# Gradient along rows: DMA issues moved from SyncE to GpSimd, row ends from GpSimd to VectorE

## The chip, the core and the metric

The kernel runs on one core of a Trainium2 chip. The metric is the device time of one execution in microseconds (us), the median of several runs. In the profile, DVE is VectorE, POOL is GpSimd, SP is SyncE, and SPq is the sequencer of SyncE that issues DMAs. 16 DMA engines move data between HBM (the input and the output) and SBUF (the memory on the core).

## The reference

```python
def setup_inputs():
    return {"x": np.random.randn(8192, 8192).astype(np.float32)}

def reference(x):
    return np.gradient(x, axis=1)
```

Along each row of 8192 values, every inner output is half the difference of its two neighbours, (x[j+1] - x[j-1]) / 2. The first output of a row is x[1] - x[0] and the last is x[8191] - x[8190], both without the half. The input is 268.4 MB and the output as much, and there is one subtraction for each value: each byte is read once and written once.

## The kernel before

The 8192 rows are worked in 32 sets. A set is 128 partitions by R = 2 rows, so that each partition holds W = 2 x 8192 values, 64 KB that lie side by side in HBM; a set is 8.39 MB. The sets come in groups of NB = 3 (the last group has two), and there are three buffers, `slot0` to `slot2`, one for each set of a group. A set is loaded to an offset of SH = 64 values in its slot, and the result is written from offset 0 of the same slot, so that the output lies behind the input that is still to be read.

Each set goes through five steps:

1. `load(i)` (line 55) brings the set in. It waits for the store of set i - 3, which used the slot before.
2. The row ends (line 65): one subtraction over four values in each partition, two for each of the two rows, into `ends`, a small tile with room for all sets. It runs on GpSimd and waits for the load.
3. The long instruction (line 71), on VectorE: half the difference of two shifted views of the whole slot, 16382 values in each partition. It ignores the borders of rows, so that the values at row ends come out wrong, and it overwrites the input. It waits for step 2.
4. The placing (line 82): a copy of the four row ends over the wrong values. It runs on VectorE for 20 of the sets, and on GpSimd for the 12 in which `i % 5` is 1 or 3 (the last two sets aside).
5. The store (line 84) takes the slot to the output; it waits for step 4.

The order on each engine is the order in which the program names its instructions (it is scheduled by hand), and an engine's queue works in that order. The three loads of the first group are issued first. After that come the steps of the three sets of a group, and once the third store of a group has been issued, the three loads of the next group follow, each after the store that frees its slot. All loads and stores stand in SyncE's queue, in this order:

```
L0 L1 L2 | S0 S1 S2 | L3 L4 L5 | S3 S4 S5 | ... | L30 L31 | S30 S31
```

The helper `chain` names the steps that an instruction has to wait for, so that the overlapping views of a slot bring in no other waits.

Of the kernel before, what the change touches and what calls it, by code (L numbers as in the profile page):

```python
# [1 line left out]

# [4 lines left out]


@with_exitstack
def kernel(  # L10
    ctx: ExitStack,
    tc: tile.TileContext,
    x: bass.AP,
    out: bass.AP,
):
    nc = tc.nc
    P = nc.NUM_PARTITIONS
    n, m = x.shape
    R = 2
    NB = 3  # L20
    SH = 64
    W = R * m
    nsets = n // (P * R)
    f32 = x.dtype

    def sets(a):
        found = []
        for first in range(0, nsets, NB):
            q = min(NB, nsets - first)
            rows = a[first * P * R : (first + q) * P * R, :].rearrange("(p q) m -> p (q m)", p=P)  # L30
            found += [rows[:, k * W : (k + 1) * W] for k in range(q)]  # L31
        return found

    x_sets, out_sets = sets(x), sets(out)

    pool = ctx.enter_context(tc.tile_pool(name="pool", bufs=1))
    pad = pool.tile([P, 32], f32, name="pad", tag="pad")
    slots = [pool.tile([P, SH + W], f32, name=f"slot{k}", tag=f"slot{k}") for k in range(NB)]
    ends = pool.tile([P, nsets, R, 2], f32, name="ends", tag="ends")
    loads, stores = [], [None] * nsets  # L40
    in_front = {}

    def chain(i, ins, *needed):
        group, engine = f"slot{i % NB}", ins.ins.engine
        keep = [o.ins for o in needed]
        if in_front.get(engine, (None,))[0] == group:
            keep.append(in_front[engine][1])
        tc.declare_no_dep(ins.ins, group=group, keep=keep, reason="implied by the needed step")
        tc.add_to_no_dep_group(group, ins.ins)
        in_front[engine] = group, ins.ins  # L50
        return ins

    def load(i):
        b = slots[i % NB]
        ins = nc.sync.dma_start(out=b[:, SH : SH + W], in_=x_sets[i])  # L55
        loads.append(chain(i, ins, *([stores[i - NB]] if i >= NB else [])))

    with tc.manual_schedule():
        for i in range(NB):
            load(i)  # L60
        for i in range(nsets):
            b = slots[i % NB]
            xin = b[:, SH : SH + W].rearrange("p (t m) -> p t m", m=m)

            ins = nc.gpsimd.tensor_sub(  # L65
                out=ends[:, i, :, :],
                in0=xin[:, :, 1 : m : m - 2],
                in1=xin[:, :, 0 : m - 1 : m - 2],
            )
            at = [chain(i, ins, loads[i])]  # L70
            ins = nc.vector._custom_dve(  # L71
                dve_ops.TENSOR_TENSOR_REDUCE_SUB_MAX,
                out=b[:, 1 : W - 1],
                in0=b[:, SH + 2 : SH + W],
                in1=b[:, SH : SH + W - 2],
                s0=0.0,
                s1=0.5,
            )
            halved = chain(i, ins, *at)
            res = b[:, 0:W].rearrange("p (t m) -> p t m", m=m)  # L80
            placer = nc.gpsimd if i % 5 in (1, 3) and i < nsets - 2 else nc.vector
            ins = placer.tensor_copy(out=res[:, :, 0 : m : m - 1], in_=ends[:, i, :, :])  # L82
            placed = chain(i, ins, halved)
            ins = nc.sync.dma_start(out=out_sets[i], in_=b[:, 0:W])
            stores[i] = chain(i, ins, placed)
            if i % NB == NB - 1:
                for k in range(i + 1, min(i + 1 + NB, nsets)):
                    load(k)


# [1 line left out]
_INS = ['x']  # L92
_OUTS = [((8192, 8192), 'float32')]


# [23 lines left out]
```

## Time and profile before

| | |
|---|---|
| time, median of 3 runs | 1245.82 us (1245.47 to 1245.9) |
| the profiled execution | 1246.23 us, of which 1244.3 us are the profile's span |
| VectorE busy | 554.6 us, 52 instructions |
| GpSimd busy | 8.9 us, 48 instructions |
| bytes moved by DMA | 536.88 MB, 431 GB/s over the span |
| long instruction on VectorE (line 71) | 32 of 17.224 us each |
| row ends on GpSimd (line 65) | 32 of 0.200 us each |
| placing on VectorE and on GpSimd (line 82) | 20 of 0.172 us and 12 of 0.192 us |
| from issue to landing, median | loads 57.9 us, stores 40.4 us |

How to read it: the span runs from the first to the last recorded instruction of one execution, and times in the timeline count from its start. A group of instructions has its line in the kernel, its engine, its output and input with their shapes, its count, its busy time and the mean of one, and the idle time of the engine ahead of it with what ended that. The time from issue to landing of a transfer includes its wait behind other transfers. A DMA record is one contiguous piece on one of the 16 engines; "GB/s" of a stretch counts the pieces that start in it, so that over a stretch of a few microseconds it can exceed what the engines carry or be zero while they are busy.

### The profile page before, as it was taken

What the parts mean: (1) busy time and instruction counts of PE and PEld (TensorE: products, weight loads), DVE (VectorE), ACT (ScalarE), POOL (GpSimd) and SP (SyncE); (2) the same over time, 40 slices, a digit from 0 to 9 for tenths busy, and PEclk for the clock granted to TensorE, in tenths of its full rate; (3) what the DMA queues carried; (4) which work ended last, traced back from release to release, by engine and by line L of the source; (5) the groups of instructions that cost most, each with busy time, mean ns of one, the idle gap of its engine ahead of it and who ended that gap; (6) DMA issues with size and microseconds to landing.
All of it is one profiled execution on the core that took longest, in us unless ns stands there. A gap on an engine that the chain in (4) does not pass through costs nothing.

```text
span 1244.3 us, 237 instructions
## 1 busy us (share of the span) xinstructions
DVE 554.6 (45%) x52; POOL 8.9 (1%) x48
## 2 busy tenths in 40 slices
DVE  2850583069009603850582079009603840591082
POOL 0000000000000000000000000000000000000000
DMA  9999999999999999999999999999999999999999
GB/s 404 438 436 423 421 438 438 438 438 436 434 423 430 434 438 438 430 436 432 428 434 436 432 436 434 438 436 430 432 428 438 436 434 438 434 434 430 430 409 404
DMA packets 9217, 536.88 MB, mean 431 GB/s; under 512 B 1024, under 2 KB 1024, under 8 KB 1024
## 3 DMA queue, kind: packets, MB, share of 16 engines
q1 hardware_dynamic: 9216, 536.88, 99.8%
q14 instruction: 1, 0.01, 0.0%
HBM read 268.44 MB, written 268.44 MB: 431 GB/s over the span
## 4 chain that ended last, share of the span: by engine, by line
another core or an unknown queue 74%; DVE 18%; DMA 3%; issue 2%; POOL 1%; SPq 0%; POOLq 0%
DVE slot L71 18%; DMA slot<-in_x_dram 3%; POOL ends L65 0%; POOL slot L82 0%; SPq L55 0%; POOLq L114 0%; DVE slot L82 0%
## 5 line engine op out<-in xcount | busy, mean ns | idle before, releaser
L71 DVE CUSTOM_DVE_ANT_0 slot<-slot 128x16382 f32<-128x16382 f32 x32 | 551.2, 17224 | 667.2 <-POOL ends L65 667.2
L65 POOL TENSOR_TENSOR ends<-slot 128x4 f32<-128x4 f32 x32 | 6.4, 200 | 988.1 <-DMA slot<-in_x_dram 988.1
L82 POOL COPY slot<-ends 128x4 f32<-128x4 f32 x12 | 2.3, 192 | 207.9 <-DVE slot L71 207.9
L82 DVE COPY slot<-ends 128x4 f32<-128x4 f32 x20 | 3.4, 172 | 0.7
L103 POOL MEMSET const-bfloat16-1.0<- 128x1 bf16 x1 | 0.1, 102 | 0.0
L103 POOL MEMSET const-uint8-127<- 128x1 uint8 x1 | 0.1, 102 | 0.0
L103 POOL MEMSET const-float32-0.0<- 128x1 f32 x1 | 0.1, 99 | 0.2 <-issue 0.2
L103 POOL MEMSET const-float32-1.0<- 128x1 f32 x1 | 0.1, 99 | 0.0
## 6 DMA issues: line engine op xcount, KB each, us to landing
slot<-in_x_dram SPq DMA_DIRECT2D x32, 57.9
out_dram<-slot SPq DMA_DIRECT2D x32, 40.4
```

What stands on the lines that cost most here:

```text
L65: ins = nc.gpsimd.tensor_sub(out=ends[:, i, :, :], in0=xin[:, :, 1 : m : m - 2], in1=xin[:, :, 0 : m - 1 : m - 2],)
L71: ins = nc.vector._custom_dve(dve_ops.TENSOR_TENSOR_REDUCE_SUB_MAX, out=b[:, 1 : W - 1], in0=b[:, SH + 2 : SH + W], in1=b[:, SH : SH + W - 2],
L82: ins = placer.tensor_copy(out=res[:, :, 0 : m : m - 1], in_=ends[:, i, :, :])
L103: nc = _bacc.Bacc("TRN2", target_bir_lowering=False, num_devices=1)
```

## The change

[...] The subtraction for the row ends and all placings run on VectorE. The order of the loads and stores among themselves, the sizes of the transfers, the slots and the waits for data stay as they were. SyncE's queue holds no transfer any more, and GpSimd's holds nothing but the 64 transfers.

```diff
     def load(i):
         b = slots[i % NB]
-        ins = nc.sync.dma_start(out=b[:, SH : SH + W], in_=x_sets[i])
+        ins = nc.gpsimd.dma_start(out=b[:, SH : SH + W], in_=x_sets[i], single_packet=True)
         loads.append(chain(i, ins, *([stores[i - NB]] if i >= NB else [])))
...
-            ins = nc.gpsimd.tensor_sub(
+            ins = nc.vector.tensor_sub(
                 out=ends[:, i, :, :],
...
             res = b[:, 0:W].rearrange("p (t m) -> p t m", m=m)
-            placer = nc.gpsimd if i % 5 in (1, 3) and i < nsets - 2 else nc.vector
-            ins = placer.tensor_copy(out=res[:, :, 0 : m : m - 1], in_=ends[:, i, :, :])
+            ins = nc.vector.tensor_copy(out=res[:, :, 0 : m : m - 1], in_=ends[:, i, :, :])
             placed = chain(i, ins, halved)
-            ins = nc.sync.dma_start(out=out_sets[i], in_=b[:, 0:W])
+            ins = nc.gpsimd.dma_start(out=out_sets[i], in_=b[:, 0:W], single_packet=True)
             stores[i] = chain(i, ins, placed)
```

## The prediction

> **What bounds the kernel now.** I read the page first, then the timeline of the first and last stretches, then busy time by stretches around the last group. The page:
>
> ```profile
> DVE 554.6 (45%) x52; POOL 8.9 (1%) x48
> ...
> DMA packets 9217, 536.88 MB, mean 431 GB/s; under 512 B 1024, under 2 KB 1024, under 8 KB 1024
> ...
> q1 hardware_dynamic: 9216, 536.88, 99.8%
> ...
> L71 DVE CUSTOM_DVE_ANT_0 slot<-slot 128x16382 f32<-128x16382 f32 x32 | 551.2, 17224 | 667.2 <-POOL ends L65 667.2
> L65 POOL TENSOR_TENSOR ends<-slot 128x4 f32<-128x4 f32 x32 | 6.4, 200 | 988.1 <-DMA slot<-in_x_dram 988.1
> L82 POOL COPY slot<-ends 128x4 f32<-128x4 f32 x12 | 2.3, 192 | 207.9 <-DVE slot L71 207.9
> L82 DVE COPY slot<-ends 128x4 f32<-128x4 f32 x20 | 3.4, 172 | 0.7
> ```
>
> One queue fills the 16 DMA engines for 99.8% of the span; VectorE is idle for more than half of it, and waits for loads (through line 65). There are 64 transfers of 8.39 MB. The 9216 records of the queue are 64 x 144: for each transfer 128 rows of 64 KB and 16 small ones, so eight rows and a small one on each engine. In the timeline two loads of a group land 19.3 us apart (139.69 and 159.01 in line 65's starts), and 64 x 19.3 = 1235 us. Everything else in the 1244.3 us span, about 9 us, is the start, the end, and transfers slower than that. Line 4 of the page puts 74% on an unknown queue: that is the same DMA time, unattributed.
>
> Start and end in the timeline (start us, length us, engine):
>
> ```profile
> 0.74 1.33 SPq L55 DMA_DIRECT2D slot<-in_x_dram  x3
> 22.77 0.20 POOL L65 TENSOR_TENSOR ends<-slot 128x4 f32<-128x4 f32 x1 [22.32 <-DMA slot<-in_x_dram]
> ...
> 1203.28 19.61 SPq L84 DMA_DIRECT2D out_dram<-slot  x2
> 1204.86 0.20 POOL L65 TENSOR_TENSOR ends<-slot 128x4 f32<-128x4 f32 x1 [19.07 <-DMA slot<-in_x_dram]
> 1205.09 17.22 DVE L71 CUSTOM_DVE_ANT_0 slot<-slot 128x16382 f32<-128x16382 f32 x1 [1.84 <-POOL ends L65]
> 1222.35 0.17 DVE L82 COPY slot<-ends 128x4 f32<-128x4 f32 x1
> ```
>
> The reader should see that nothing stands ahead of the first load, and that the store of set 30 is issued at 1203.28, only 1.6 us before the last load lands. Busy time by stretches there (stretch, length, DVE, POOL, clock, DMA share, GB/s started):
>
> ```profile
> 1203.30:1204.10 0.80, 0.00 (x0) 0.00 (x0) 1.00 0.00 0
> 1204.10:1204.30 0.20, 0.00 (x0) 0.00 (x0) 1.00 11.49 4915
> 1204.30:1204.45 0.15, 0.00 (x0) 0.00 (x0) 1.00 0.00 0
> 1204.45:1204.60 0.15, 0.00 (x0) 0.00 (x0) 1.00 1.01 437
> ```
>
> 4915 GB/s x 0.20 us = 983 KB: 15 rows, on 15 engines together, 0.85 us after the issue. The sixteenth row starts some 0.35 us behind them, on the engine that was still busy with the load. So at this one place the queue runs dry: 15 engines wait for the issue, and the slowest has 0.35 us of cover.
>
> **The change part by part.** The 64 DMA issues go from SP's queue to GpSimd's, in the same order. SP is left empty, and nothing is moved past an instruction that took time there. The 32 differences (line 65) and the 12 copies of line 82 leave GpSimd, so no compute stands in front of an issue on its queue.
>
> Row ends: VectorE gains 32 differences of about 0.20 us (GpSimd's row; its own 128x4 copies take 0.17) and 12 copies of 0.17, 8.4 us in all. A set then takes it 0.20 + 17.22 + 0.17 = 17.6 us plus short gaps, against a load every 19.3 us, and it rests 60 us in each group. All of this hides under transfers except in the last two sets, where the hop from GpSimd costs 0.23 us now (1204.86 to 1205.09) and the difference on VectorE about as much: 0, bounds -0.1 and +0.1 per set. The new wait is that the difference of set i+1 waits for its load in VectorE's order. Ahead of it stands the copy of set i, behind it only work on set i+1, which needs that load anyway: no cost. Without the cover of transfers the price would be the 8.4 us.
>
> GpSimd's issue waits: a refill of a slot waits for its store to land, and the next group's stores queue behind. The third refill of a group waits longest, to about 120.5 us in the first group (81.69 + 39), and the store behind it is ready at 157.4: 37 us of room.
>
> Issue to first row: SP takes 1.0 us at the start (0.74 to the rows of 1.7 to 1.8) and 0.85 us at set 30's store. No row here shows a transfer issued by GpSimd. Nearest rows: SP's own path, and GpSimd's smallest instructions, 0.1 to 0.2 us. Below: no more than on SP, +0 (it is the same kind of request). Above: two more of SP's whole path, +2.0 us. I take one more of it, +1.0 us, since software on GpSimd has to write out 128 rows before an engine starts. The Trainium skill, "DMA: Bandwidth & Descriptors", Specifications, gives first-byte times of about 1 us from GpSimd and 0.6 us from SP; by that difference of 0.4 us the sum below would be an estimated +0.45 in place of +1.65. No run here shows it yet.
>
> Where that +1.0 lies: at the first load it is open, +1.0. In the steady groups it is covered: set 3's store is issued at 157.43 and the loads ahead of it keep the engines busy to the landing at 178.6, 21 us of room. At set 30's store it is open but for the 0.35 us: +0.65. Set 31's store (issued 1222.55, 1203.28 + 0.85 + 19.3 = 1223.4 is when the first engines come free) shifts by the same amount, not once more.
>
> [...] What there is to save is at most the difference between the mean transfer, 99.8% of 1244.3 us / 64 = 19.40 us, and the shortest landing step, 19.27 (1185.59 to 1204.86): 64 x 0.13 = 8 us, of which about 1 us is the first transfer's start-up: -7 us. To cost, packets would have to stop overlapping; a store takes at least 20.9 us from issue to landing where the transfer itself takes 19.3, so 1.6 us each, +100 us as the far end. With the engines already busy 99.8%, the row nearest to this kernel's queue says back to back: I take 0.
>
> End of the program: GpSimd may have to close 64 transfers of its own; no row shows it. Below 0, above 64 x 0.1 us (its shortest instruction) = 6.4 us; I take 0, because before's queue ends about a microsecond after its last row.
>
> Sum: +1.0 + 0.65 + 0 + 0 = +1.65 us. The profiled execution took 1246.23 us (span 1244.3 and 1.9 around it), which gives 1247.9; it lies 0.4 above the median of the runs, 1245.82, which gives 1247.5, 0.13% more than before. A measurement of this kernel can tell about 0.2%, 2.5 us, from no change, so the likeliest outcome is no difference that can be told, on the slow side.
>
> **The rivals.** (1) Latency or closing dearer than taken: +2.0 at the start, +1.65 at the tail, up to 6.4 at the end, together up to +10, or 1255.9. It decides from 2.5 us on, that is from an issue path 1.45 us longer than SP's. For: both open places are certain, and nothing prices GpSimd's path from above. Against: nothing in the trace asks for so much.
>
> (2) VectorE holds GpSimd's descriptor writing up. Set 30's store is issued 1.8 us before VectorE starts its 17.2 us instruction on set 31 (1203.28, 1205.09). If the writing isn't done by then and has to wait for 1222.3, the store starts 18 us late and the last transfer behind it: +18 and +1.0 at the start, 1264.8. In the steady groups the same delay just fits into the 21 us of room. Against: 1.8 us is more than the path I take, and the long instruction must exclude GpSimd at all; in this trace no GpSimd instruction runs beside one, so it shows neither. The Trainium skill, "SBUF — State Buffer", Who interferes with whom, says that GpSimd can't write descriptors while VectorE runs in a mode with two ports, and that an instruction with two SBUF inputs takes only the read side; by that, line 71 would not block and the short copies would, for 0.17 us. No run here shows it yet.
>
> (3) The path itself moves bytes more slowly, for all 64 transfers. The poorest inner slices of the page hold 421 GB/s against the mean of 431: 536.88 MB at the one and the other is 1275.2 and 1245.7 us, +30, or 1275. It decides from 0.04 us per transfer on. Against: the engines are busy and the bytes are the same. The skill's page on DMA, Measured, has 425 GB/s for large loads issued from GpSimd, by which it would be an estimated +18.
>
> (4) Faster: the packets take the spread out, -7 + 1.65 = -5.3, 1240.5. For: line 65 starts 20.31 us apart in sets 1 and 2 (42.03, 62.34), and up to 19.8 at the same place of later groups. Against: the first step of a group, and each of the four transfers between two groups (77.3 us together), are within 0.1 us of the shortest already.
>
> **How the numbers follow.** Forecast case 0.44; rival 1 0.27; rival 2 0.06; rival 3 0.12; rival 4 0.11. That the change doesn't do what it says can be left at none: every issue stands on GpSimd's queue. The forecast case alone spans 1244 to 1248.3. The range leaves out rivals 2 and 3 (0.18) and reaches from rival 4's 1240.5 to rival 1's 1255.9. Faster by over 0.2% 0.11, within 0.44, slower 0.27 + 0.06 + 0.12 = 0.45.
>
> **What would show it.** In the profile after: the first load's landing (22.77 now) about 1 us later; line 71's idle time still ended by loads; landings in a group still 19.3 us apart; the stretch without rows ahead of set 30's store longer by about 1 us; VectorE busy about 563 us. Landing steps of 19.35 or more speak for rival 3, of 19.2 for rival 4; a first row of set 30's store only at 1222 for rival 2; a long piece between the last row and the end of the span for the closing in rival 1. The prediction is wrong if steady landing steps move by over 0.04 us, or if the stores of a steady group leave the engines idle.

## The result and the profile after

The changed kernel takes 1250.8 us, median of 5 runs (1250.25 to 1251.39), beside 1245.82 us for the kernel before (1245.18 to 1245.94). The ratio is 1.0041, with a 95% interval of 1.0027 to 1.0054: slower by 5.0 us. A second series of the same kernel gave 1251.57 against 1246.17, 1.0042 [1.0029, 1.0055]. The forecast was 1247.5, in a range of 1240.5 to 1255.9. The profiled execution took 1250.25 us (span 1248.5), the lowest of its series; that of before, at 1246.23 us, lies above all of its five.

The page of the changed kernel, the lines that answer to those shown of before:

```profile
DVE 561.9 (45%) x96; POOL 34.4 (3%) x68
...
DMA packets 9218, 536.89 MB, mean 430 GB/s; under 512 B 1024, under 2 KB 1024, under 8 KB 1024
...
q0 software_dynamic: 9216, 536.88, 99.5%
...
L71 DVE CUSTOM_DVE_ANT_0 slot<-slot 128x16382 f32<-128x16382 f32 x32 | 551.2, 17223 | 1.1
L65 DVE TENSOR_TENSOR ends<-slot 128x4 f32<-128x4 f32 x32 | 5.3, 165 | 659.6 <-DMA slot<-in_x_dram 659.6
L83 POOL DMA_DIRECT2D out_dram<-slot x32 | 17.1, 535 | 818.2 <-DVE slot L81 818.2
L55 POOL DMA_DIRECT2D slot<-in_x_dram x32 | 17.1, 535 | 371.6 <-DMA out_dram<-slot 370.8
L81 DVE COPY slot<-ends 128x4 f32<-128x4 f32 x32 | 5.5, 171 | 1.1
```

Everything is on queue q0 now, the pieces are as many and as large, and the DMA engines are busy for 99.5% of the span. The row ends cost VectorE 0.165 and 0.171 us each. The 64 issues, which were not counted as work on SP, appear as 34 us of work on GpSimd, 0.535 us each. Nothing here names a loss of 5 us; most of it lies at the two ends of the timeline:

```profile
1.27 1.72 POOL L55 DMA_DIRECT2D slot<-in_x_dram  x3 [0.82 <-PEq L113]
23.52 0.17 DVE L65 TENSOR_TENSOR ends<-slot 128x4 f32<-128x4 f32 x1 [23.52 <-DMA slot<-in_x_dram]
...
1186.74 0.16 DVE L65 TENSOR_TENSOR ends<-slot 128x4 f32<-128x4 f32 x1 [59.65 <-DMA slot<-in_x_dram]
...
1204.20 0.17 DVE L81 COPY slot<-ends 128x4 f32<-128x4 f32 x1
1204.66 0.54 POOL L83 DMA_DIRECT2D out_dram<-slot  x1 [55.76 <-DVE slot L81]
1206.04 0.17 DVE L65 TENSOR_TENSOR ends<-slot 128x4 f32<-128x4 f32 x1 [1.67 <-DMA slot<-in_x_dram]
```

The first load has landed at 23.52 and not at 22.77. A landing is read here from the start of the instruction that waits for it. The load of set 30 lands at 1186.74, 1163.22 us after the first; before, it was 1185.59 - 22.77 = 1162.82. Busy time by stretches at set 30's store:

```profile
1204.37:1205.55 1.18, 0.00 (x0) 0.54 (x1) 1.00 0.00 0
1205.55:1205.65 0.10, 0.00 (x0) 0.00 (x0) 1.00 0.00 0
1205.65:1205.80 0.15, 0.00 (x0) 0.00 (x0) 1.00 7.16 3058
1205.80:1206.50 0.70, 0.43 (x2) 0.00 (x0) 1.00 1.97 843
```

From the end of the copy (1204.37) to the first row, which the trace has at 1205.77, it takes 1.40 us; before it took 0.88 (1203.25 to 1204.13). 3058 x 0.15 and 843 x 0.70 are 7 and 9 rows of 65.5 KB: all 16 engines begin here. The last rows of the load end at 1205.70 in the trace, so that the slowest engine too stands dry, for 0.1 to 0.2 us. Before, its row of the load ended at 1204.51 and its row of the store began at 1204.52.

The largest part comes after the last byte. The last line of the program in the view of one line's instructions, and the waits of SP:

```profile
L113 POOLq DRAIN  x3: 40/89/23815, 1223.9 to 1248.2; - x3
L113 SPq DRAIN  x3: 7/7/7, 1245.2 to 1248.0; - x3
```

```profile
SPq L113 <- DMA out_dram<-slot: 39.0, 2, 19.6
SPq L113 <- PEq L113: 3.1, 2, 2.7
```

DRAIN is the profile's name for an instruction near the end of an engine's queue. SP has seen the last store land when its DRAIN runs, at 1245.2. GpSimd's DRAIN begins with the last issue, at 1223.94, and takes 23.815 us, until 1247.76: 2.66 us longer than to the landing, which the trace has at 1245.10. All engines wait for it, which is the 2.7 us of SP's second line. Before, the same two rows read

```profile
L114 POOLq DRAIN  x3: 34/76/302, 1204.8 to 1244.1; - x3
L114 SPq DRAIN  x3: 7/7/7, 1243.6 to 1243.9; - x3
```

and GpSimd had long been idle. The account of the pair of profiles, from the landings in the traces: first landing +0.75; from there to the load of set 30 +0.40; from that to the last landing 58.35 against 57.90, +0.45; from the last landing to the meeting of the engines 2.71 against 0.17, +2.54. The sum is 4.1 of the 4.2 us between the spans. The third of these terms is not the issue path alone: the slowest engine stood dry for 0.1 to 0.2 us of it, and where the rest lies is not shown.

### The profile page after: what moved, and what is told of

It reads as the page before. It is cut to its first block, busy times and chain, and to the rows that moved or that the text cites. A ratio compares the mean times of both kernels' runs of the same rounds, so it can differ in the third digit from the quotient of the medians.

```text
span 1248.5 us, 234 instructions
## 1 busy us (share of the span) xinstructions
DVE 561.9 (45%) x96; POOL 34.4 (3%) x68
## 3 DMA queue, kind: packets, MB, share of 16 engines
q0 software_dynamic: 9216, 536.88, 99.5%
## 4 chain that ended last, share of the span: by engine, by line
another core or an unknown queue 41%; DVE 37%; issue 11%; DMA 10%; POOL 0%; POOLq 0%; PEldq 0%
DVE slot L71 36%; DMA out_dram<-slot 6%; DMA slot<-in_x_dram 3%; DVE ends L65 0%; DVE slot L81 0%; POOL slot L55 0%; POOLq L113 0%; POOL out_dram L83 0%; POOLq L83 0%; PEldq L113 0%; POOLq L55 0%
## 5 line engine op out<-in xcount | busy, mean ns | idle before, releaser
L65 DVE TENSOR_TENSOR ends<-slot 128x4 f32<-128x4 f32 x32 | 5.3, 165 | 659.6 <-DMA slot<-in_x_dram 659.6
L83 POOL DMA_DIRECT2D out_dram<-slot x32 | 17.1, 535 | 818.2 <-DVE slot L81 818.2
L55 POOL DMA_DIRECT2D slot<-in_x_dram x32 | 17.1, 535 | 371.6 <-DMA out_dram<-slot 370.8
```

The source lines that it names most:

```text
L55: ins = nc.gpsimd.dma_start(out=b[:, SH : SH + W], in_=x_sets[i], single_packet=True)
L65: ins = nc.vector.tensor_sub(out=ends[:, i, :, :], in0=xin[:, :, 1 : m : m - 2], in1=xin[:, :, 0 : m - 1 : m - 2],)
L83: ins = nc.gpsimd.dma_start(out=out_sets[i], in_=b[:, 0:W], single_packet=True)
```

## The experiments

All were timed against the kernel before. The theory at the outset was three fixed places: a later first row at the start, the same at the tail, and the closing of GpSimd's queue. Its rivals were the row ends on VectorE, the packet flag (`single_packet=True` in both calls), and a slower path for each transfer.

**Row ends alone** (e1_ends_only). Edit, against the changed kernel:

```diff
-ins = nc.gpsimd.dma_start(out=b[:, SH : SH + W], in_=x_sets[i], single_packet=True)
+ins = nc.sync.dma_start(out=b[:, SH : SH + W], in_=x_sets[i])
...
-ins = nc.gpsimd.dma_start(out=out_sets[i], in_=b[:, 0:W], single_packet=True)
+ins = nc.sync.dma_start(out=out_sets[i], in_=b[:, 0:W])
```

> The row ends run on VectorE as in the changed kernel, all 64 transfers are issued by SP as before. If moving the row ends is free, as the prediction has it, the time is that of before, 1245.8 us within 1 us, with SP's last wait ending near 1243.6 us. If VectorE's extra 44 small instructions, or their waits, are what costs, the time is near the changed kernel's 1250.8.

Measured: 1245.56 against 1245.54, 1.0 [0.9991, 1.0009]. Within the interval, about 1 us, moving the row ends is free, and the loss belongs to the issue path.

**No packet flag** (e2_no_packet): `single_packet=True` taken out of both calls, GpSimd still issues.

> The changed kernel without single_packet. Theory (the cost lies in GpSimd's issue path at the start and the tail, and in closing its queue at the end): no difference, 1250.8 within 1 us, GpSimd's long DRAIN at the end still about 2.5 us longer than the last landing. Rival (the packet flag itself costs, in the closing or in the pace): 1247 to 1249, and the DRAIN ends with the last landing.

Measured: 1250.68 against 1245.54, 1.0041 [1.0028, 1.0053]; the DRAIN ends 2.66 us after the last landing, as with the flag.

**The packet flag on SP** (e8_sp_packet): the kernel of row ends alone with `single_packet=True` in both calls.

> All 64 transfers through SP, as single packets, row ends on VectorE. Theory (the packet flag changes nothing for rows of 64 KB): the time of before, 1245.5 within 1 us. Rival (packets save the overhead between rows on SP's path): 1243 to 1244.5.

Measured: 1245.94 against 1246.22, 0.9999 [0.9991, 1.0008]. On neither path does the flag make a difference that can be told, with rows of 64 KB. In the profiles the number of records stays 9216 for the queue with and without it; what the flag does to the rows of a transfer no run here shows.

**The last two stores on SP** (e3_last2_sp):

```diff
+on_sp = i >= nsets - 2
-ins = nc.gpsimd.dma_start(out=out_sets[i], in_=b[:, 0:W], single_packet=True)
+ins = (nc.sync if on_sp else nc.gpsimd).dma_start(
+    out=out_sets[i], in_=b[:, 0:W], single_packet=not on_sp)
```

> The changed kernel, but the last two stores go through SP. GpSimd's last transfer is then the load of set 31, which lands 38 us before the end. Theory (closing the queue starts once GpSimd's last transfer has landed and is hidden under other transfers): the 2.6 us at the end and the 0.4 us at the tail's issue go, 1247 to 1248 us, span about 1245.5. Rival (the closing costs the same wherever the last transfer stands, because it is only started by the end of the program): about 1250. Second rival (the loss is spread over the 62 transfers in between): about 1250.5.

Measured: 1248.96 against 1245.54, 1.0027 [1.0016, 1.0038]. The closing is out of the way, as the view of the last line shows:

```profile
L114 POOLq DRAIN  x3: 40/88/60212, 1149.6 to 1247.3; - x3
L114 SPq DRAIN  x3: 7/7/7, 1246.8 to 1247.1; - x3
```

From 1149.56 and 60.212 us long, the DRAIN ends at 1209.77, 37 us ahead of SP's, and the last landing is followed by the end of the span after 0.8 us. But the time is 1 to 2 us above what the theory gave. A part of that stands where the queues meet: in the trace the last engine's first row from SP's queue, behind a load from GpSimd's, takes 3.16 us in place of 2.42, here and in the next kernel, and that engine ends 1 us behind the other fifteen (1246.28, the others by 1245.31). That the change of queue makes the row slow is argued from these two traces. Rows of more than 3 us occur in the middle of every trace with rows of 64 KB; after 1150 us these two kernels alone have one.

**Both ends of the run on SP** (e4_ends_of_run_sp): the edit above, and `on_sp = i < NB` for the loads.

> The first three loads and the last two stores go through SP, the 59 transfers in between through GpSimd as single packets. Theory (three places: start 0.75, tail 0.4 to 0.7, closing 2.6, and nothing in between): the time of before, 1245.8 within 1 us. Rival (the path is slower for each transfer): 59 of 64 parts of the 5 us stay, 1250.

Measured: 1247.56 against 1245.54, 1.0017 [1.0008, 1.0026], +2.0 us. Both expectations were missed. The three places hold most of the 5 us, but with them taken out something of 1 to 3 us is left. The first landing is back at 22.55. The slow row is 0.74 us longer than the others, and the load of set 30 lands 1163.29 us after the first, 0.5 more than before.

**The last loads on SP too** (e9_ends_and_last_loads_sp): `on_sp = i < NB or i >= nsets - 2` for the loads.

> The first three loads, the last two loads and the last two stores go through SP, 57 transfers in between through GpSimd; the closing of GpSimd's queue starts some 40 us before the end. What is told apart: what remained of the loss when only the last stores were on SP (2.0 us, of which about 1 us was one engine that finished late). If that came from stores on SP behind a load on GpSimd, 1245.5 to 1246.5 here. If it is spread over GpSimd's transfers, 1247.5 again.

Measured: 1247.92 against 1246.17, 1.0013 [1.0004, 1.0022]. It is nearer to the second case, but does not settle it: the two queues take turns here from 1130 to 1202 us, and 13 of the rows that start between 1160 and 1210 take 2.54 to 2.84 us.

**One transfer of GpSimd** (e5_only_last_store_gp): loads by SP; for the stores `on_sp = i < nsets - 1`.

> SP issues 63 transfers, GpSimd only the very last store; row ends on VectorE. What is told apart: is the 2.6 us that GpSimd's DRAIN runs on after the last landing a fixed price, or so much for each transfer of the queue? Fixed: DRAIN ends 2.5 us after the last landing, time 1248.5 to 1249. For each transfer (2.6 / 64 = 0.04 us): DRAIN ends with the landing, time 1246 to 1246.5 (the later issue of one store, 0.4).

Measured: 1246.61 against 1246.22, 1.0002 [0.9994, 1.0011]; the 0.4 us between the medians are those of the second case.

```profile
L114 POOLq DRAIN  x3: 34/88/21190, 1222.9 to 1244.6; - x3
L114 SPq DRAIN  x3: 7/7/7, 1244.1 to 1244.4; - x3
```

The DRAIN starts at 1222.89, ends at 1244.09, and the landing was at 1244.01. With one transfer in the queue the closing takes 0.08 us; a fixed price of 2.6 us is ruled out.

**The last 16 on GpSimd** (e6_last16_gp): `on_sp = i < 24` for loads and stores.

> The first 48 transfers go through SP, the last 16 (sets 24 to 31) through GpSimd as single packets. Fixed closing: DRAIN ends 2.6 us after the last landing, time 1248.5 to 1249.3. Closing for each transfer: 0.65 us after it, time 1246.7 to 1247.3. Against the changed kernel (1250.8) the start's 0.75 is gone in both cases; if some of the loss is spread over the transfers, 48 of 64 parts of that are gone too.

Measured: 1249.87 against 1246.22, 1.0028 [1.0017, 1.004]: slower than either case had it. The DRAIN (1225.98 and 21.848 us) ends 0.70 us after the last landing at 1247.13, which is the price for each transfer. The time was lost elsewhere. The page's speeds in 40 slices have one poor slice near the end, where GpSimd's transfers follow SP's:

```profile
GB/s 403 437 437 437 434 426 426 426 437 437 437 434 434 434 432 432 430 428 434 432 434 437 437 437 437 437 434 428 432 437 430 397 430 437 437 437 437 434 409 370
```

The 397 stands in the slice from 968 to 999 us, and the load of set 30 lands at 1188.80, 3.2 us later than before. That the change of queues made this loss is argued from one trace, and the kernel of row ends alone, which has no such change, has slices of 413 too. So the time of this kernel decides nothing; its closing does.

**128 transfers in place of 64** (e7_halves):

```diff
-ins = nc.gpsimd.dma_start(out=b[:, SH : SH + W], in_=x_sets[i], single_packet=True)
+for h in range(R):
+    ins = nc.gpsimd.dma_start(out=b[:, SH + h * m : SH + (h + 1) * m],
+                              in_=x_sets[i][:, h * m : (h + 1) * m], single_packet=True)
```

and the stores in the same way.

> The changed kernel with every load and store cut into two of 32 KB rows, 128 transfers through GpSimd in place of 64. Fixed closing: DRAIN ends 2.6 us after the last landing; closing for each transfer: 5.2 us after it, and the time 2.6 us higher from this alone, about 1253.5. The smaller rows may cost some more in the pace of the transfers, which the landings in the profile show apart from the closing.

Measured: 1253.9 against 1246.22, 1.0063 [1.0049, 1.0077]. The time is near what was expected, for another reason: the closing was 0.94 us, which neither case had. The 3 us above the changed kernel come from the pace: the load of set 30 lands 1168.09 us after the first, 4.9 us more, with 16 rows of 32 KB on an engine in place of 8. GpSimd's own timeline shows where the rest of the closing may have gone:

```profile
1058.86 0.54 POOL L57 DMA_DIRECT2D slot<-in_x_dram  x1 [2.50 <-issue]
```

Once, after 113 issues, GpSimd stands still for 2.5 us with nothing to wait for, and the engines have work queued meanwhile. An estimate from the rows: 0.94 / 0.041 = 23 transfers were left at the end, about the 15 issued after that pause and the 5 in flight then. But closing the 108 that had landed would take 108 x 0.041 = 4.4 us by the same price, and the pause is 2.5. That the queue was closed once on the way is argued, not shown.

**The order of the last transfers** (e11_sp_last_loads_first, and e12_gp_last_loads_first for the changed kernel):

```diff
+if i == nsets - 3:
+    load(i + 1)
+    load(i + 2)
 ins = nc.sync.dma_start(out=out_sets[i], in_=b[:, 0:W])
```

> All transfers on SP, row ends on VectorE, and the loads of sets 30 and 31 are issued ahead of the store of set 29, so that this store fills the time in which VectorE works on set 30. Theory (at set 30's store the queue runs dry on 15 engines, and only the slowest engine sets the end): the dry stretch goes, and the time falls by the 0.3 us of the slowest engine at most, 1245 to 1245.6. Rival (the dry stretch costs its mean of 1.7 us): 1244.

> The changed kernel with the loads of sets 30 and 31 issued ahead of the store of set 29. Theory: the later issue at the tail (0.45 us) is now covered, the start's 0.75 and the closing's 2.6 stay: 1249.8 to 1250.4. Rival (the tail's issue costs more than the profile shows): 1249 or less.

Measured: on SP 1246.33 against 1246.17, 1.0002 [0.9993, 1.0011]; on GpSimd 1250.73 against 1246.17, 1.0037 [1.0024, 1.005]. In both the queue never runs dry, and neither gains anything that can be told; both lie above their forecasts. The second is 0.8 us below the unedited kernel of the same series (1251.57, the next experiment), with runs that overlap. So it neither confirms nor refutes that the dry stretch costs 0.45. The last stretches of the two, SP first:

```profile
1240.00:1242.00 2.00, 0.00 (x0) 0.00 (x0) 1.00 0.15 66
1242.00:1244.00 2.00, 0.00 (x0) 0.00 (x0) 1.00 0.00 0
```

```profile
1240.00:1242.00 2.00, 0.00 (x0) 0.00 (x0) 1.00 0.38 164
1242.00:1244.00 2.00, 0.00 (x0) 0.00 (x0) 1.00 0.23 98
```

Without the dry stretch, at which the other engines wait for the slowest, the slowest engines stand out: 66 x 2.0 is two rows that start after 1240 on SP's path, and 164 x 2.0 and 98 x 2.0 are five and three on GpSimd's, the three of them after 1242. In these two traces the last row ends 2.4 us after the first engine is done on SP's path, and 4.5 us after it on GpSimd's. The pair shows more than the medians do (6.1 us between the spans, 4.4 between the medians): SP's profiled execution was the shortest of its eleven (1245.56), GpSimd's the longest of its five (1251.71).

**The changed kernel again** (e10_changed_again), unedited:

> The changed kernel once more, beside the others of this call: 1250.8 within 0.7 us; in the profile the first landing at 23.5, the DRAIN's end 2.6 us after the last landing.

Measured: 1251.57 against 1246.17, just outside what was expected; first landing 23.74, DRAIN 2.66 us after the last landing.

The closing over all kernels, as the end of GpSimd's DRAIN less the last landing in its own queue: 0.08 us with 1 transfer, 0.70 with 16, 2.38 with 57, 2.46 with 59, 2.58 with 62, 2.66 with 64. That is (2.66 - 0.08) / 63 = 0.041 us for each transfer. The kernel with 128 transfers, at 0.94, stands outside this row.

## Why the prediction was right, and where it was not

The range held and the forecast case did not. A difference too small to tell was put first, at 0.44; what came is rival 1, at 0.27.

**What bounds the kernel** held: one full DMA queue. The four transfers from a group's last load to the next group's first take 77.31 us on the mean in both profiles.

**Row ends** at 0: shown by their own run, within its interval (1.0 [0.9991, 1.0009]). **GpSimd's waits** in the steady groups at 0: the third refill's issue at 122.06 stood 36 us ahead of the next store, as the 37 us of room had it.

**Start**, +1.0 forecast: +0.75 at the landing in this pair of profiles, and 0.98 between the means of all traces (22.50 to 22.83 in the eight with the first loads on SP, 23.52 to 23.74 in the six with them on GpSimd). The size was right. The place was right in part: GpSimd's first issue itself begins 0.53 us later (1.27 against 0.74), and from that issue to the first row, where the forecast had the whole of it, the pair has 1.38 against 1.01 us. What holds the first issue up by 0.53 us no run told apart.

**Tail**, +0.65 forecast: +0.45, and 0.42 to 0.47 between any of three traces of each kind. From the copy's end to the first row the path is 0.52 us longer than SP's, where the forecast took 1.0. The cover of 0.35 us was there as forecast: 0.52 less the cover leaves the slowest engine dry for 0.1 to 0.2 us, as the trace has it, and the rest of the 0.45 is not placed. The Trainium skill's difference of 0.4 us between first-byte times ("DMA: Bandwidth & Descriptors", Specifications) is near both the 0.37 from the first issue on and the 0.52 here.

**The packet flag** at 0: shown by two kernels for the time. No run shows what the flag does to a transfer; the records are as many with it as without.

**End of the program** was the term that was mis-sized: forecast 0 between bounds of 0 and 6.4, measured +2.54. The reason given, that before's queue ends about a microsecond after its last row, was a row of SP's queue; GpSimd had issued nothing there, so it could not carry the choice. The upper bound was built rightly, one small piece of work for each of 64 transfers, but priced at 0.1 us where it takes 0.041. With 2.54 in its place and 0.98 and 0.45 for start and tail, the sum is 4.0 us, or 1249.8, beside the measured 1250.8; the 1 us of the next paragraph is what is missing.

**What remains** is about 1 us and is spread. From the first landing to that of set 30's load, the four kernels with these transfers on SP (before, e1, e5, e8) took 1162.34 to 1163.16 us (mean 1162.7), and four with all of them on GpSimd (the changed kernel twice, e2, e3) 1163.22 to 1164.21 (mean 1163.7). In the traces it shows most on a few engines. In those of the changed kernel, its repeat and the kernel without the flag, the last two engines post the landing of set 30's load 1.2, 2.6 and 2.1 us behind the other fourteen; in the four traces on SP the fifteenth follows the fourteenth after 0.04 to 0.83 us. In the fourth trace on GpSimd (e3) three engines are behind. The cause is open: no run told apart why these engines fall behind. The section "Latency and other measured facts" of the Trainium skill's page "DMA: Bandwidth & Descriptors" says that two of the 16 engines are usually slower, and suspects the descriptors that GpSimd keeps in SBUF. Two is the number in the first three of these traces, not in the fourth. The records do not name the engine, so no run here can show the rest.

**The rivals.** Rival 1 is what happened, "latency or closing dearer than taken", by the closing and not by the latency. (By its own terms it decides from an issue path 1.43 us longer than SP's on, 2 x 1.43 - 0.35 = 2.5, not 1.45.) Rival 2 did not come: GpSimd's issue of set 30's store was over at 1205.20, a microsecond before VectorE's long instruction, so the case in which the two overlap was not tried, here or in any other run. Rival 3's 0.04 us per transfer was not reached: 1 us in 60 transfers is 0.017, and the page of the changed kernel has 430 GB/s against 431 before. Rival 4 was excluded by the two kernels without and with the flag.

## What to carry to other kernels

Here, moving the DMA issues to another engine changed neither the bytes nor the number of pieces that the DMA engines carry, and most of the loss lay at the ends. So price the two ends of the run: the first transfer, any place where the queue runs dry, and what the engine still has to do after its last transfer has landed. An engine whose row shows it idle in the profile before says nothing about the end of the program when it gets work; look for its DRAIN against the last landing. If GpSimd must issue transfers, let another queue issue the last ones and check the landings: with the last two stores on SP 1.7 of the 5 us were gone (1248.96 against 1250.68 in the same series), and with the first three loads there as well 3 us. But in the kernel that changed queues in the middle the load of set 30 landed 3.2 us late.

## What was not expected of the hardware

GpSimd's DRAIN runs on after the last landing by 0.041 us for each transfer of its queue since the start, as long as there are no more than 64 (0.08 us with 1, 2.66 with 64). With 128 it was 0.94, and what happened on the way is open. In the kernels of up to 64 the work was not done while the queue waited: between issues GpSimd was idle for 1190 us (818.2 and 371.6).

Where the queues changed, two traces have one row of 3.16 us, on an engine that goes from GpSimd's transfer to SP's, and one trace has a slice of 397 GB/s where GpSimd's transfers follow SP's. That the change made them is argued from these few traces.
